# Scaled copies out of the gates' banks, and three pieces of side work moved by a few tiles

## The chip, the cores and the metric

The kernel runs on one core of a Trainium2 chip. The metric is the device time of one execution, in microseconds (us). A core has five engines that run their own instruction queues in order: PE (matmuls; its weight loads are listed as PEld), DVE (elementwise work on tensors), ACT (activations, copies, casts), POOL (here memsets and masks) and SP (here it only starts DMAs). They wait for each other by semaphores.

## The reference

One decoder layer on 256 tokens of width 2048, all float32. The parts that the change touches:

```python
h = rmsnorm(x, norm_gain[l])
z = h @ w_in[l]
(gq, gk_, gv, ggate, gdown, fq, fk, fv, flogit, fgate, mq, mgate, merge) = jnp.split(z, IN_OFFSETS, axis=-1)
gk_log = jax.nn.log_sigmoid((gdown @ w_gk_up[l] + b_gk[l]).astype(jnp.float32)) / GK_NORMALIZER
o_a = gla_chunked(...)                                   # gated linear attention, 4 heads of 256
o_a = rmsnorm(o_a, gla_norm_gain[l]).reshape(B, S, GLA_WIDTH).astype(x.dtype)
o_a = o_a * jax.nn.silu(ggate)
log_f = jax.nn.log_sigmoid((flogit + b_f[l]).astype(jnp.float32))
o_b = forgetting_attention(...) * jax.nn.silu(fgate)
mkv = rmsnorm(mem, mem_norm_gain[l]) @ w_mem_kv[l]       # 256 memory tokens
o_c = memory_attention(...) * jax.nn.silu(mgate)
gates = jax.nn.sigmoid(merge.reshape(B, S, N_BRANCH, D))
y = gates[:, :, 0] * (o_a @ wb_a) + gates[:, :, 1] * (o_b @ wb_b) + gates[:, :, 2] * (o_c @ wb_c)
x = x + y @ w_out[l]
return rmsnorm(x, final_gain)
```

Here `gdown` has 16 columns and `flogit` 8: these 24 are the "small columns". Norms are not applied to x or mem before the products: the products are made with the raw x times the gain, and their results are scaled afterwards by the token's reciprocal root mean square (`xcol`, `xrow` for x, `mcol`, `mrow` for the memory tokens; a column has a token on a partition, a row has the tokens along the free axis, the same on all partitions).

## The kernel before

The 2048 input rows are 16 tiles of 128, the "kts". All large weights are streamed in 34 blocks of 2048 rows by 512 columns, in the fixed order of a table: gq, gk, gv (two blocks), fq, fk, fv, the memory's k and v, mq, ggate (two blocks), fgate, mgate, then four times three merge blocks and one block of the branches, and four blocks of the output projection. A float32 weight is loaded (`raw`), cast to a high part by ACT (`hi`, L174, in the first block L130), and the rest is subtracted by DVE (`lo`, L187, in the first block L131). Each product is made of three: high by high, high by low, low by high. The casts and subtractions work in pieces of two kts, which run three and two pieces ahead of PE. The first block is special: x itself comes with it, so `first_piece` (L376) loads x and weights piece by piece, and splits both.

Blocks are computed in two ways. `natural` (L211) has the tokens on the partitions: for each kt and each of the two token tiles three matmuls, into two PSUM banks (L224 to L226). `transposed` (L232) has the columns on the partitions, four banks: in groups of four kts each bank c in turn gets a 512-wide matmul (L255) and a 256-wide one (L257) for each kt; at the end a bank is emptied by an ACT copy (L240) and a DVE addition (L243). There are four `acc` banks for these blocks and four `att` banks for the rest (and for gq, which is in groups of one kt). A block that follows reuses the banks of the one before it, so its first matmul on a bank waits for whoever empties that bank.

All other work is written as generators in three lanes, `post`, `side` and `main`. After each kt (in groups of four: after each bank's turn) `pull` advances each lane by one step. A generator that yields n is taken up again n pulls later. So the numbers in `yield` fix where an instruction stands in its engine's queue, and since each lane is a list, what follows in a lane moves with it.

The change touches these: `small` (L411), first in the side lane: splits the small columns `wsr` in two halves of eight kts (L422, L423) and multiplies them (L431: eight matmuls for kts 0 to 7, then four, then four); `wsr` and the 16 rows of the low-rank weight `w3r` are loaded in `first_piece` (L398 to L400). After it in the side lane stand the scale of x (`scale_first`, L502), the loads and splits of the memory tokens (`load_mem`, L365), and the memory tokens' scale: `rms_of` (L298: four squares on ACT, L308; then the sums on DVE, L311 and L312; then `rsqrt`, L285, with Ln and Exp on ACT, each of which needs a table load, L290 and L291) and `row_of` (L315: a DVE multiplication of the identity, L319, a matmul by ones, L322, a copy). In the main lane `gla_decay` (L526) makes three stacked copies `z3` of the small result and multiplies them (L543); the scores with L658, L661 and L662 follow. `silu_gate` (L895) is for the two ggate blocks: natural product, then `evac`, a sigmoid of the scaled PSUM bank by ACT (L902, with a table load ahead of it), the product of bank, scale and sigmoid by DVE (L904, which frees the bank), and four products with the attention's result (L910).

Of the kernel before, what the change touches and what calls it, by code (L numbers as in the profile page):

```python
# [12 lines left out]
AF = mybir.ActivationFunctionType  # L13
ALU = mybir.AluOpType
AX = mybir.AxisListType

P = 128
# [43 lines left out]
def body(ctx, tc, xT, memT, xn, memn, wall, wsm, wup, cst, fgain, out):  # L61
# [250 lines left out]
        nc.vector.tensor_scalar(ms, ms, 4.0 / D, 4 * EPS, ALU.mult, ALU.add)  # L312
        yield from rsqrt(col, ms, NT)

    def row_of(col, row):  # L315

        dg = a2([P, NT, P])
        for t in range(NT):
            nc.vector.tensor_scalar(dg[:, t, :], ident, col[:, t:t + 1], None, ALU.mult)  # L319
        yield 2  # L320
        ps = att()
        MM(ps[:, :S], lhsT=ones, rhs=dg.rearrange("p t s -> p (t s)"), start=True, stop=True)  # L322
        yield 1
        nc.scalar.copy(row, ps[:, :S])
        yield 1
# [53 lines left out]
    def first_piece(g, s, raw, hi, lo):  # L379

        if s == 0:
            xraws.append(a4([P, 4, S]))
            x12.append(new_h("x12_", g))
        step = 1 if g < 2 else 2
        for k in range(0, 2, step):
            ks = slice(2 * s + k, 2 * s + k + step)
            kts = slice(4 * g + ks.start, 4 * g + ks.stop)
            nc.sync.dma_start(xraws[g][:, ks, :], xT[:, kts, :])
            cut = (0, 256, NB) if kts.start == 0 else (0, NB)
            for a, b in zip(cut, cut[1:]):  # L390
                nc.sync.dma_start(raw[:, ks, a:b], wall[0, :, kts, a:b])
            for j in range(ks.start, ks.stop):
                kt = 4 * g + j
                high_x(x12[g], xraws[g][:, j, :], j, cs[:, C_GAIN + kt:C_GAIN + kt + 1])
                low_x(x12[g], xraws[g][:, j, :], j, cs[:, C_GAIN + kt:C_GAIN + kt + 1])
                for a, b in zip(cut, cut[1:]):
                    split_w(raw[:, j, a:b], hi[:, j - 2 * s, a:b], lo[:, j - 2 * s, a:b])
        if (g, s) == (1, 1):  # L398
            nc.sync.dma_start(wsr, wsm)
            nc.sync.dma_start(w3r, wup)  # L400

# [8 lines left out]
    def small():  # L410

        for g in range(2):
            z0 = a4([P, 8, P], F32)
            nc.gpsimd.memset(z0, 0.0)
            ws = a4([P, 8, P], F32R)
            nc.gpsimd.tensor_copy(ws, z0)
            zs.append(ws)
        yield 3
        for g in range(2):
            ws, wr = zs[g], wsr[:, 8 * g:8 * g + 8, :]  # L420
            for (a, b, wdt) in ((0, 0, 16), (32, 16, 8)):
                nc.vector.tensor_copy(ws[:, :, a:a + wdt], wr[:, :, b:b + wdt])  # L422
                nc.vector.tensor_tensor(out=ws[:, :, 64 + a:64 + a + wdt], in0=wr[:, :, b:b + wdt],  # L423
                                        in1=ws[:, :, a:a + wdt].bitcast(F32), op=ALU.subtract)
            yield 3
        nc.scalar.copy(w3, w3r)
        nc.vector.tensor_tensor(out=w3[32:64], in0=w3r[32:64], in1=w3[32:64].bitcast(F32), op=ALU.subtract)
        sp = acc()
        for kts, n in ((range(0, 8), 3), (range(8, 12), 4), (range(12, 16), 1)):
            for kt in kts:  # L430
                MM(sp, lhsT=zs[kt // 8][:, kt % 8, :], rhs=h_of(x12, kt).rearrange("p a s -> p (a s)"),  # L431
                   start=(kt == 0), stop=(kt == KT - 1))
            yield n
        nc.scalar.copy(sm, sp[0:64, S:])
        nc.vector.tensor_tensor(out=sm, in0=sp[0:64, :S], in1=sm, op=ALU.add)
        nc.vector.tensor_tensor(out=sm, in0=sp[64:128, :S], in1=sm, op=ALU.add)
        yield 1
# [89 lines left out]
    def gla_decay():  # L527
# [7 lines left out]
        nc.scalar.copy(z3[0:32], sm[0:32])  # L535
        nc.scalar.copy(z3[32:64], sm[0:32])
        nc.vector.tensor_tensor(out=z3[64:96], in0=sm[0:32], in1=z3[0:32].bitcast(F32), op=ALU.subtract)
        yield 1
        for c in range(2):
            ps = att()  # L540
            for j in range(2):
# [353 lines left out]
    def silu_gate(dst, rstd):  # L895
# [1 line left out]
        ps = natural(x12, range(KT), w_kts(w_block()))  # L897

        def evac():
            sgs = [a2([P, NB]) for _ in range(NT)]  # L900
            for t in range(NT):
                nc.scalar.activation(sgs[t], ps[t], AF.Sigmoid, scale=xcol[:, t:t + 1])  # L902
            for t in range(NT):
                nc.vector.scalar_tensor_tensor(out=sgs[t], in0=ps[t], scalar=xcol[:, t:t + 1], in1=sgs[t],  # L904
                                               op0=ALU.mult, op1=ALU.mult)
                yield 1
            for t in range(NT):
                for j in range(2):
                    sl = slice(j * 256, (j + 1) * 256)
                    nc.vector.scalar_tensor_tensor(out=dst(t)[:, sl], in0=dst(t)[:, sl],  # L910
                                                   scalar=rstd()[:, t, j:j + 1], in1=sgs[t][:, sl],
                                                   op0=ALU.mult, op1=ALU.mult)
                yield 1
            yield 1

        return evac()

# [26 lines left out]
    side.append(load_mem())  # L944
    side.append(gap(10))
    side.append(rms_of(memn, mcol, lambda: a4([P, 1024])))
    side.append(row_of(mcol, mrow))
    G["k"] = proj_T(x12, scaled(lambda: G["row"]))
    main.append(gla_decay())
    main.append(gla_scores())  # L950
# [258 lines left out]
```

## Time and profile before

| what | value |
| --- | --- |
| median of three runs | 817.73 us (817.65 to 817.75) |
| profiled execution | 817.97 us, of which the span of the instructions is 816.0 us |
| mean granted clock of PE | 0.998 |
| PE busy | 802.0 us (98%) in 3888 matmul records |
| DVE / ACT / POOL busy | 499.4 (61%) / 408.6 (50%) / 22.1 us (3%) |
| HBM | 154.55 MB read, 192 GB/s over the span |

In rows of the timeline the first number is the start in us from the start of the span, the second the duration in us; then come the engine, the line of the kernel, the operation, what it writes and reads, shapes and types, how many instructions are put together in the row, and in square brackets the idle time of the engine just before it and who ended it. In the list of waits: who waited for whom, us in total, how often, the longest in us. In a table of windows a row has the stretch, its length, the busy time (and number of instructions) of PE, PEld, DVE, ACT and POOL, then the granted clock of PE (1.00 is full speed), the busy share of the DMA engines and GB/s. In a group of instructions: how many, busy us and mean ns of one, idle us before.

### The profile page before, as it was taken

What the parts mean: (1) busy time and instruction counts of PE and PEld (TensorE: products, weight loads), DVE (VectorE), ACT (ScalarE), POOL (GpSimd) and SP (SyncE); (2) the same over time, 40 slices, a digit from 0 to 9 for tenths busy, and PEclk for the clock granted to TensorE, in tenths of its full rate; (3) what the DMA queues carried; (4) which work ended last, traced back from release to release, by engine and by line L of the source; (5) the groups of instructions that cost most, each with busy time, mean ns of one, the idle gap of its engine ahead of it and who ended that gap; (6) DMA issues with size and microseconds to landing.
All of it is one profiled execution on the core that took longest, in us unless ns stands there. A gap on an engine that the chain in (4) does not pass through costs nothing.

```text
span 816.0 us, 9964 instructions
## 1 busy us (share of the span) xinstructions
PE 802.0 (98%) x3888; PEld 673.0 (82%) x3888; DVE 499.4 (61%) x705; ACT 408.6 (50%) x560; POOL 22.1 (3%) x44
## 2 busy tenths in 40 slices
PE   8999999999999999999999999999999999999995
PEld 7888888788888787888888888888888888888885
DVE  6767978875756575567445644474446544575653
ACT  6777745744645464555444444434444444444631
POOL 6000010100000000000000000000000000000000
PEclk9999999999999999999999999999999999999999
DMA  8965646643444443555555455555555555548633
GB/s 294 368 235 181 239 158 237 213 161 130 180 155 156 156 153 123 187 182 186 200 206 187 173 206 197 178 193 203 180 188 203 183 184 200 206 161 308 233 125 103
DMA packets 27439, 157.31 MB, mean 193 GB/s; under 512 B 3216, under 2 KB 4640, under 8 KB 10496
## 3 DMA queue, kind: packets, MB, share of 16 engines
q1 hardware_dynamic: 27120, 156.64, 54.0%
q8 instruction: 30, 0.49, 0.2%
q14 instruction: 17, 0.14, 0.0%
q10 hardware_dynamic: 144, 0.02, 0.0%
q0 software_dynamic: 128, 0.02, 0.0%
HBM read 154.55 MB, written 2.10 MB: 192 GB/s over the span
## 4 chain that ended last, share of the span: by engine, by line
PE 60%; DVE 1%; ACT 0%; DVEq 0%; issue 0%
PE acc L226 14%; PE acc L224 14%; PE acc L225 14%; PE acc L1073 4%; PE acc L1074 4%; PE acc L1075 4%; PE acc L255 3%; PE acc L257 2%; PE att L986 0%; PE att L844 0%; DVE b L904 0%; DVE lo L187 0%; PE att L888 0%; PE att L853 0%; PE att L862 0%; ACT b L902 0%
## 5 line engine op out<-in xcount | busy, mean ns | idle before, releaser
L187 DVE TENSOR_TENSOR lo<-raw,hi 128x1024 fp32r<-128x1024 f32 x256 | 312.2, 1223 | 199.7 <-ACT hi L174 199.5
L174 ACT CAST hi<-raw 128x1024 fp32r<-128x1024 f32 x256 | 265.8, 1050 | 318.0 <-PE acc L226 237.9
L224 PE MATMUL acc<-hi,x 128*128 128x512 f32 x544 | 215.2, 396 | 0.0
L225 PE MATMUL acc<-lo,x 128*128 128x512 f32 x544 | 212.1, 390 | 0.0
L226 PE MATMUL acc<-hi,x 128*128 128x512 f32 x544 | 212.1, 390 | 0.0
L255 PE MATMUL acc<-x,hi 128*128 128x512 f32 x384 | 138.9, 404 | 1.3 <-DVE b L904 1.2
L226 PEld LDWEIGHTS acc<-hi,x 128*128 128x128 f32 x544 | 102.1, 188 | 21.6
L225 PEld LDWEIGHTS acc<-lo,x 128*128 128x128 f32 x544 | 102.2, 188 | 21.0 <-DVE lo L187 0.5
L224 PEld LDWEIGHTS acc<-hi,x 128*128 128x128 f32 x544 | 102.2, 188 | 21.0 <-issue 0.3
L257 PE MATMUL acc<-x,lo 128*128 128x256 f32 x384 | 107.3, 280 | 0.0
L255 PEld LDWEIGHTS acc<-x,hi 128*128 128x128 f32 x384 | 72.1, 188 | 18.4 <-DVE b L904 1.9
L257 PEld LDWEIGHTS acc<-x,lo 128*128 128x128 f32 x384 | 72.4, 189 | 0.5 <-DVE lo L187 0.2
L226 PE MATMUL acc<-hi,oT 128*128 128x512 f32 x128 | 49.8, 389 | 0.0
L225 PE MATMUL acc<-lo,oT 128*128 128x512 f32 x128 | 49.8, 389 | 0.0
L224 PE MATMUL acc<-hi,oT 128*128 128x512 f32 x128 | 49.8, 389 | 0.0
L1073 PE MATMUL acc<-hi,a 128*128 128x512 f32 x96 | 37.6, 391 | 0.0
L1075 PE MATMUL acc<-hi,a 128*128 128x512 f32 x96 | 37.4, 390 | 0.0
L1074 PE MATMUL acc<-lo,a 128*128 128x512 f32 x96 | 37.4, 389 | 0.0
L225 PEld LDWEIGHTS acc<-lo,oT 128*128 128x128 f32 x128 | 24.0, 188 | 5.0
L226 PEld LDWEIGHTS acc<-hi,oT 128*128 128x128 f32 x128 | 24.0, 188 | 5.0
L224 PEld LDWEIGHTS acc<-hi,oT 128*128 128x128 f32 x128 | 24.0, 188 | 5.0
L255 PE MATMUL att<-x,hi 128*128 128x512 f32 x64 | 24.1, 415 | 0.6 <-ACT hi L130 0.6
(223 smaller groups left out, 803.2 us busy)
## 6 DMA issues: line engine op xcount, KB each, us to landing
raw<-wall SPq DMA_DIRECT2D x130, 1024.0 KB, 4.7
a<-xn SPq DMA_DIRECT2D x8, 512.0 KB, 7.2
raw<-wall SPq DMA_DIRECT2D x4, 512.0 KB, 6.9
a<-memT SPq DMA_DIRECT2D x4, 512.0 KB, 7.4
a<-memn SPq DMA_DIRECT2D x4, 512.0 KB, 7.5
lraw<-wall SPq DMA_DIRECT2D x2, 1024.0 KB, 7.4
out<-a SPq DMA_DIRECT2D x8, 256.0 KB, 3.1
raw<-wall SPq DMA_DIRECT2D x7, 256.0 KB, 4.8
```

The lines of the kernel that those rows point to most:

```text
L174: nc.scalar.copy(hi, raws[q][:, 2 * s:2 * s + 2, :])
L187: nc.vector.tensor_tensor(out=lo, in0=raws[q][:, 2 * s:2 * s + 2, :], in1=parts[n][0].bitcast(F32), op=ALU.subtract)
L224: MM(ps[t], lhsT=h1, rhs=hi, start=(kt == first), stop=False)
L225: MM(ps[t], lhsT=h1, rhs=lo, start=False, stop=False)
L226: MM(ps[t], lhsT=h2, rhs=hi, start=False, stop=(kt == last))
L255: MM(ps[c], lhsT=hi[:, cs_], rhs=hk.rearrange("p a s -> p (a s)"), start=(kt == 0), stop=False, skip_group_check=True)
L257: MM(ps[c][:, :S], lhsT=lo[:, cs_], rhs=hk[:, 0, :], start=False, stop=(kt == KT - 1), skip_group_check=True)
L1073: MM(ps, lhsT=h1, rhs=hi, start=(kt == 0), stop=False)
L1074: MM(ps, lhsT=h1, rhs=lo, start=False, stop=False)
L1075: MM(ps, lhsT=h2, rhs=hi, start=False, stop=(kt == KT - 1))
```

## The change

Five edits. In `row_of` the distance between the DVE multiplication and the matmul becomes a parameter, 2 as before for the tokens' scale and 6 for the memory tokens'. In `first_piece` the loads of the small columns move from behind the piece of kts 6 and 7 to behind the piece of kts 10 and 11. In `small` the splits are six pulls after the start rather than three, and one pull apart rather than three, which makes the side lane one pull shorter up to the matmuls L431. In `gla_decay` the matmuls come two pulls after the copies rather than one, and all of the main lane behind them one pull later. In `evac` of the gates the bank is emptied by an ACT copy with the scale (a Copy needs no table here), the product with the attention's result is made from that copy, and the sigmoid is taken of the copy in place afterwards and multiplied in.

```diff
--- before.py
+++ after.py
@@ -312,12 +312,12 @@
         nc.vector.tensor_scalar(ms, ms, 4.0 / D, 4 * EPS, ALU.mult, ALU.add)
         yield from rsqrt(col, ms, NT)
 
-    def row_of(col, row):
+    def row_of(col, row, wait=2):
 
         dg = a2([P, NT, P])
         for t in range(NT):
             nc.vector.tensor_scalar(dg[:, t, :], ident, col[:, t:t + 1], None, ALU.mult)
-        yield 2
+        yield wait
         ps = att()
         MM(ps[:, :S], lhsT=ones, rhs=dg.rearrange("p t s -> p (t s)"), start=True, stop=True)
         yield 1
@@ -395,7 +395,7 @@
                 low_x(x12[g], xraws[g][:, j, :], j, cs[:, C_GAIN + kt:C_GAIN + kt + 1])
                 for a, b in zip(cut, cut[1:]):
                     split_w(raw[:, j, a:b], hi[:, j - 2 * s, a:b], lo[:, j - 2 * s, a:b])
-        if (g, s) == (1, 1):
+        if (g, s) == (2, 1):
             nc.sync.dma_start(wsr, wsm)
             nc.sync.dma_start(w3r, wup)
 
@@ -415,14 +415,14 @@
             ws = a4([P, 8, P], F32R)
             nc.gpsimd.tensor_copy(ws, z0)
             zs.append(ws)
-        yield 3
+        yield 6
         for g in range(2):
             ws, wr = zs[g], wsr[:, 8 * g:8 * g + 8, :]
             for (a, b, wdt) in ((0, 0, 16), (32, 16, 8)):
                 nc.vector.tensor_copy(ws[:, :, a:a + wdt], wr[:, :, b:b + wdt])
                 nc.vector.tensor_tensor(out=ws[:, :, 64 + a:64 + a + wdt], in0=wr[:, :, b:b + wdt],
                                         in1=ws[:, :, a:a + wdt].bitcast(F32), op=ALU.subtract)
-            yield 3
+            yield 1
         nc.scalar.copy(w3, w3r)
         nc.vector.tensor_tensor(out=w3[32:64], in0=w3r[32:64], in1=w3[32:64].bitcast(F32), op=ALU.subtract)
         sp = acc()
@@ -535,7 +535,7 @@
         nc.scalar.copy(z3[0:32], sm[0:32])
         nc.scalar.copy(z3[32:64], sm[0:32])
         nc.vector.tensor_tensor(out=z3[64:96], in0=sm[0:32], in1=z3[0:32].bitcast(F32), op=ALU.subtract)
-        yield 1
+        yield 2
         for c in range(2):
             ps = att()
             for j in range(2):
@@ -897,21 +897,23 @@
         ps = natural(x12, range(KT), w_kts(w_block()))
 
         def evac():
-            sgs = [a2([P, NB]) for _ in range(NT)]
+            zs = [a2([P, NB]) for _ in range(NT)]
             for t in range(NT):
-                nc.scalar.activation(sgs[t], ps[t], AF.Sigmoid, scale=xcol[:, t:t + 1])
-            for t in range(NT):
-                nc.vector.scalar_tensor_tensor(out=sgs[t], in0=ps[t], scalar=xcol[:, t:t + 1], in1=sgs[t],
-                                               op0=ALU.mult, op1=ALU.mult)
-                yield 1
+                nc.scalar.activation(zs[t], ps[t], AF.Copy, scale=xcol[:, t:t + 1])
+            yield 2
             for t in range(NT):
                 for j in range(2):
                     sl = slice(j * 256, (j + 1) * 256)
                     nc.vector.scalar_tensor_tensor(out=dst(t)[:, sl], in0=dst(t)[:, sl],
-                                                   scalar=rstd()[:, t, j:j + 1], in1=sgs[t][:, sl],
+                                                   scalar=rstd()[:, t, j:j + 1], in1=zs[t][:, sl],
                                                    op0=ALU.mult, op1=ALU.mult)
                 yield 1
-            yield 1
+            for t in range(NT):
+                nc.scalar.activation(zs[t], zs[t], AF.Sigmoid)
+            yield 2
+            for t in range(NT):
+                nc.vector.tensor_tensor(out=dst(t), in0=dst(t), in1=zs[t], op=ALU.mult)
+                yield 1
 
         return evac()
 
@@ -944,7 +946,7 @@
     side.append(load_mem())
     side.append(gap(10))
     side.append(rms_of(memn, mcol, lambda: a4([P, 1024])))
-    side.append(row_of(mcol, mrow))
+    side.append(row_of(mcol, mrow, 6))
     G["k"] = proj_T(x12, scaled(lambda: G["row"]))
     main.append(gla_decay())
     main.append(gla_scores())
```

How the order of the instructions changes is shown at three places. The first is DVE in the first block: L351 is the low part of x, L131 that of the weights (two of each per piece of two kts), L422 and L423 the splits of `wsr`, first half `a_191` (now `a_189`), second half `a_195` (now `a_193`). Before:

```order
L351 SCALAR_TENSOR_TENSOR x_30_209<-a_208,cs,x_30_209 128x256
L131 TENSOR_TENSOR lo_207<-raw_205,hi_206 128x512
L422 CAST a_191<-wsr 128x8x16
L423 TENSOR_TENSOR a_191<-wsr,a_191 128x8x16
L422 CAST a_191<-wsr 128x8x8
L423 TENSOR_TENSOR a_191<-wsr,a_191 128x8x8
L351 SCALAR_TENSOR_TENSOR x_30_209<-a_208,cs,x_30_209 128x256
L131 TENSOR_TENSOR lo_241<-raw_205,hi_240 128x512
```

and now, where `lo_266` is the piece of kts 12 and 13:

```order
L351 SCALAR_TENSOR_TENSOR x_37_268<-a_267,cs,x_37_268 128x256
L131 TENSOR_TENSOR lo_266<-raw_264,hi_265 128x512
L422 CAST a_189<-wsr 128x8x16
L423 TENSOR_TENSOR a_189<-wsr,a_189 128x8x16
L422 CAST a_189<-wsr 128x8x8
L423 TENSOR_TENSOR a_189<-wsr,a_189 128x8x8
L422 CAST a_193<-wsr 128x8x16
L423 TENSOR_TENSOR a_193<-wsr,a_193 128x8x16
L422 CAST a_193<-wsr 128x8x8
L423 TENSOR_TENSOR a_193<-wsr,a_193 128x8x8
```

The first half's split stood behind kt 9's low parts and now stands behind kt 13's, with the second half's right after it. On PE the first eight matmuls L431 stand behind kt 8, where they stood behind kt 9:

```order
L255 MATMUL att_184<-x_30_207,hi_204 128x512
L257 MATMUL att_184<-x_30_207,lo_205 128x256
L431 MATMUL acc_331<-x_8_114,a_189 128x512 x4
L431 MATMUL acc_331<-x_15_148,a_189 128x512 x4
L255 MATMUL att_175<-x_30_207,hi_204 128x512
L257 MATMUL att_175<-x_30_207,lo_205 128x256
```

The second place is ACT at the end of the fk block, where the memory tokens' scale is made: L308 are the squares, L240 the copies that empty fk's banks (`acc_1280` the first, `acc_1295` the second; now `acc_1280` and `acc_1296`), L290 and L291 the Ln and Exp with their table loads. Before:

```order
L308 ACTIVATE a_1424,ssq_1306<-a_1424 128x1024
L662 ACTIVATE a_1464<-a_1464 128x768
L240 COPY a_1275<-acc_1280 128x256
L308 ACTIVATE a_1426,ssq_1306<-a_1426 128x1024
L240 COPY a_1275<-acc_1295 128x256
L290 ACT_TABLE_LOAD
L290 ACTIVATE nwp_1520<-ms_1517 128x2
L291 ACT_TABLE_LOAD
L291 ACTIVATE nwp_1520<-nwp_1520 128x2
L240 COPY a_1275<-acc_1311 128x256
```

and now:

```order
L658 ACTIVATE a_1449<-a_1449 128x1024
L308 ACTIVATE a_1402,ssq_1289<-a_1402 128x1024
L240 COPY a_1275<-acc_1280 128x256
L290 ACT_TABLE_LOAD
L290 ACTIVATE nwp_1504<-ms_1501 128x2
L291 ACT_TABLE_LOAD
L291 ACTIVATE nwp_1504<-nwp_1504 128x2
L662 ACTIVATE a_1477<-a_1477 128x768
L240 COPY a_1275<-acc_1296 128x256
L240 COPY a_1275<-acc_1311 128x256
```

The last square now stands ahead of the first copy, and both table loads with L662 ahead of the second. The third place is ACT at the end of the second ggate block (`acc_2627` and `acc_2628`, now `acc_2625` and `acc_2626`). Before:

```order
L174 CAST hi_2838<-raw_2713 128x1024
L902 ACT_TABLE_LOAD
L902 ACTIVATE b_2849<-acc_2627,xcol 128x512
L902 ACTIVATE b_2850<-acc_2628,xcol 128x512
L174 CAST hi_2897<-raw_2771 128x1024
```

and now:

```order
L174 CAST hi_2838<-raw_2703 128x1024
L902 ACTIVATE b_2849<-acc_2625,xcol 128x512
L902 ACTIVATE b_2850<-acc_2626,xcol 128x512
L868 ACTIVATE b_2826,msum<-att_2825,mmx 128x256 x2
L174 CAST hi_2895<-raw_2758 128x1024
L174 CAST hi_2897<-raw_2758 128x1024
L912 ACT_TABLE_LOAD
L912 ACTIVATE b_2849<-b_2849 128x512
L912 ACTIVATE b_2850<-b_2850 128x512
```

The table load and the sigmoids have moved behind two casts, and only copies stand between the block's end and the free banks.

## The prediction

> **What bounds the kernel now.** I read the page first, then the waits of PE, then the timeline around each of them.
>
> ```profile
> span 816.0 us, 9964 instructions
> PE 802.0 (98%) x3888; PEld 673.0 (82%) x3888; DVE 499.4 (61%) x705; ACT 408.6 (50%) x560; POOL 22.1 (3%) x44
> PE 60%; DVE 1%; ACT 0%; DVEq 0%; issue 0%
> PE att L322 <- DVE b L319: 1.4, 1, 1.4
> PE acc L255 <- DVE b L904: 1.2, 1, 1.2
> PE att L255 <- ACT hi L130: 0.6, 1, 0.6
> PE att L257 <- DVE lo L131: 0.4, 2, 0.2
> PE att L543 <- ACT hi L174: 0.2, 1, 0.2
> ```
>
> PE is busy for 802.0 of 816.0 us, and the chain of waits lies on it. The change neither adds nor removes a matmul, so only PE's stalls can move. The four lines of waits below L322's, and that one, are the places the change touches; all of them together hold about 4 us. Any stall that the change makes is paid in full, since nothing behind PE has to catch up.
>
> **The change, part by part.**
>
> *A. The small columns.* Their loads go two pieces back and the first half's splits eight DVE instructions back, while the small matmuls L431 come one kt earlier on PE.
>
> ```profile
> 8.98 0.48 SPq L399 DMA_DIRECT2D wsr<-wsm  x1
> 10.71 0.43 SPq L388 DMA_DIRECT2D a<-xT  x1
> 14.07 0.33 SPq L391 DMA_DIRECT2D raw<-wall  x1
> 17.26 0.28 PE L257 MATMUL att<-x,lo 128*128 128x256 f32 x1
> 21.41 0.62 ACT L130 CAST hi<-raw 128x512 fp32r<-128x512 f32 x1
> 22.35 0.61 ACT L130 CAST hi<-raw 128x512 fp32r<-128x512 f32 x1
> 23.95 0.69 DVE L131 TENSOR_TENSOR lo<-raw,hi 128x512 fp32r<-128x512 f32 x1
> 19.73 0.22 DVE L422 CAST a<-wsr 128x128 fp32r<-128x128 f32 x1
> 20.42 0.23 DVE L423 TENSOR_TENSOR a<-wsr,a 128x64 fp32r<-128x64 f32 x1
> 21.57 2.00 PE L431 MATMUL acc<-x,a 128*128 128x512 f32 x8
> 23.41 0.39 PE L255 MATMUL att<-x,hi 128*128 128x512 f32 x1
> 27.64 1.08 PE L431 MATMUL acc<-x,a 128*128 128x512 f32 x4
> ```
>
> Today SP issues wsr's load at 8.98 and wup's after it, so the xT of kts 8 and 9 is issued only at 10.71. Without those two, kt 8's data comes 10.71 − 8.98 = 1.7 us sooner, and the stall before kt 8 (0.6 for the cast, some 0.2 twice for lo) goes: kt 7's last matmul starts at 17.26, and kt 8 would run from about 17.4 to 18.8 (one kt takes (27.64 − 23.41)/3 = 1.41). That is the gain meant.
>
> Behind kt 8, however, L431 now stands, and it needs the first half's split of wsr. On DVE this split has moved behind the lo pieces up to kt 13. So PE waits for kt 13's weights before it may do kt 9, which is ready. Kt 12 and 13's weights are issued at 14.07 today; the two loads moved still stand ahead of them, so they come no earlier. ACT casts kt 12 at 21.41 and kt 13 at 22.35, ending 22.96. Then lo of kt 13 (0.69, to 23.7) and the split of the first half (19.73 to 20.65: 0.92) follow, to 24.6, and L431 starts at about 24.7. If lo of kt 13 stays where it is today (23.95) it is 25.6; if the casts come half a microsecond earlier, 24.1.
>
> L431 started at 21.57 with kts 8 and 9 done; now it starts at 24.7 with kt 8 alone done. So A costs (24.7 − 21.57) + 1.41 = **+4.5 us** (3.9 to 5.4), the removed stall counted in. PE then stands idle for 24.7 − 18.8 = 5.9 us, where DVE and ACT work on, so all later splits lie readier than today and no further stall follows. The second half's split comes right behind and is ready by 25.6; its four matmuls stand three kts later.
>
> *The clock.* So long an idle stretch brings the granted clock in.
>
> ```profile
> 1.13 3.35 PE L343 MATMUL att<-ones 128*128 128x128 f32 x14 [1.13 <-DVE ones L335]
> 5.24 0.63 PE L255 MATMUL att<-x,hi 128*128 128x512 f32 x1
> 7.04 0.40 PE L255 MATMUL att<-x,hi 128*128 128x512 f32 x1
> 807.02 0.28 PE L1075 MATMUL acc<-last,a 128*128 128x256 f32 x1
> 812.00:812.50 0.50, 0.00 (x0) 0.00 (x0) 0.00 (x0) 0.00 (x0) 0.00 (x0) 0.92 1.00 279
> 812.50:814.00 1.50, 0.00 (x0) 0.00 (x0) 0.00 (x0) 0.00 (x0) 0.00 (x0) 0.50 0.60 202
> ```
>
> The last matmul ends at 807.3. The granted clock (the column before the last two) is 0.92 on average from 812.0 to 812.5 and 0.50 after, so it fell at 812.4, 5.1 us after the end of work. At the start, matmuls run from 1.13; a 512-wide one still takes 0.63 at 5.24 and 0.40 at 7.04, so full speed came some 5 to 6 us after the first. An idle stretch of 5.9 us is longer than 5.1, so I expect the clock to halve just before L431. Slow work costs about 1 − 0.40/0.63 = 37% to half of its time, say 45%. Five and a half slow microseconds would cost 2.5; as L431 follows soon after the fall and the first slow period at the start followed no earlier work, between half of it and all: **+2.0** (0, if the clock does not fall in time, to 2.8).
>
> The Trainium skill, page "TensorE: Matmul & The Clock Gate", section "Part 1: The HAM clock gate (the "warmup" mystery)", has the gate closed by a whole idle window of about 3.4 us and opened by a busy one, the windows running free. By that rule 5.9 us of idle hold a whole window in (5.9 − 3.4)/3.4, about 70%, of all alignments, and the closed clock lasts one to two windows, an estimate of 1.5 to 3 us lost; the 5.1 us at the end agree with it.
>
> *B. The memory tokens' scale.* L322 now stands three kts further back on PE, so its wait of 1.4 goes. But the side lane is one step earlier in all that follows the small columns, and the table loads of mcol's rsqrt now stand ahead of a copy that frees a bank.
>
> ```profile
> 146.14 2.00 ACT L174 CAST hi<-raw 128x1024 fp32r<-128x1024 f32 x2 [0.44 <-PE acc L255]
> 148.04 1.06 ACT L308 ACTIVATE a<-a 128x1024 f32<-128x1024 f32 x1
> 148.37 1.22 DVE L661 TENSOR_TENSOR a<-a,a 128x1024 f32<-128x1024 f32 x1
> 149.10 0.83 ACT L662 ACTIVATE a<-a 128x768 f32<-128x768 f32 x1
> 150.64 0.42 DVE L243 TENSOR_TENSOR a<-acc,a 128x256 f32<-128x256 f32 x1
> 151.13 0.35 ACT L240 COPY a<-acc 128x256 f32<-128x256 f32 x1
> 151.51 1.28 ACT L290 ACT_TABLE_LOAD   x1
> 153.02 1.28 ACT L291 ACT_TABLE_LOAD   x1
> 152.26 0.39 PE L224 MATMUL acc<-hi,x 128*128 128x512 f32 x1
> 153.01 0.19 PEld L224 LDWEIGHTS acc<-hi,x 128*128 128x128 f32 x1 [0.33 <-DVE a L243]
> ```
>
> Today both copies L240 of fk's first two banks are done by 151.5, ahead of the loads, and fv's second bank opens at 153.01 with a wait of 0.33. In the new order ACT does, from the end of the two casts at 148.1 (bound by PE, so they stay): L308, L658, L308 (1.06 each, L658 of the same shape, to 151.3), L240 (0.35, to 151.65), the loads with Ln and Exp (from the start of the first load today to the end of the second 153.02 + 1.28 − 151.51 = 2.8, and Exp with it some 3.0, to 154.6), L662 (0.83, to 155.4), and only then the second L240 (to 155.8). DVE's L243 (0.42) then opens fv's second bank at about 156.2. DVE itself stands at L311 until the last L308, then L661 and a lo (1.22 each) keep the first bank's L243 until 154.6; PE waits there first, from 152.26, and the rest of the wait at the second bank. So the second bank opens at 156.2 in place of 153.0: +3.2 − 1.4 = **+1.8 us** (from −1.4, if the loads hide as they do today, to +2.4).
>
> *C. The gates.* Today a table load and two sigmoids from PSUM stand before L904, which frees the banks.
>
> ```profile
> 316.63 1.28 ACT L902 ACT_TABLE_LOAD   x1
> 319.44 0.50 PE L255 MATMUL acc<-x,hi 128*128 128x512 f32 x1 [1.17 <-DVE b L904]
> 321.24 0.19 PEld L255 LDWEIGHTS acc<-x,hi 128*128 128x128 f32 x1 [0.45 <-DVE b L904]
> L471 ACT ACTIVATE a<-acc,xcol 128x512 f32<-128x512 f32 x6 | 4.0, 678 | 0.0
> ```
>
> The scaled copy is of the form of L471, 0.68 each. From 316.63 the copies free the banks at 317.3 and 318.0; PE wants the first at 319.44 − 1.17 = 318.3 and the second later. Both waits go, 1.17 + 0.45: **−1.6 us** (0, if something else keeps the banks, to −1.6). The table load, the sigmoids in place (four more ACT instructions in all, 0.68 each by the same row) and the multiplication by DVE come later, beside PE's next block; ACT is busy for 50% of the span, and the transposes that want the result stand kts later. Without that cover a late result would cost what the gate's chain grows by, 2 × 0.68 and a second DVE pass, about 2 us.
>
> *D. The decay's matmuls* L543 move one kt back; their wait of 0.2 goes: **−0.2**. The rest of main's lane goes one kt later with them, which moves work past other banks' copies, at no more than ±0.5 by the size of the waits quoted.
>
> Sum: 4.5 + 2.0 + 1.8 − 1.6 − 0.2 = +6.5. The profiled execution took 817.97 us (span 816.0), 0.24 over the median 817.73, so 824.5 in its own time and **824.2 us** beside the median.
>
> **The rivals.** *First, the bank is not held:* ACT reaches the loads with time to spare because fk's banks fill later than I place them, and B is −1.4. For it: L308 waits for nothing today. Against it: the order puts 3.0 us of table work straight ahead of a copy that PE stands 0.33 behind already. 817.7 + 4.5 + 2.0 − 1.4 − 1.6 − 0.2 = 821.0.
>
> *Second, the clock does not fall:* idle time and fall lie 0.8 us apart, and the end of the program may differ from its middle. For that: one fall only is on the trace. Against: the three times agree within 0.1 us, though each holds a slow start where each microsecond of shift would show as 0.4; so the clock's steps do not wander. 824.2 − 2.0 = 822.2; with B gained too 819.0, close to no difference.
>
> *Third, the clock's whole price and late ends everywhere:* L431 at 25.6, 2.8 slow: 817.7 + 5.4 + 2.8 + 1.8 − 1.6 − 0.2 = 825.9.
>
> *Fourth, on the other side, the change does what it says:* the split of wsr is not late, for instance since PE's wait is released by an earlier count than that behind kt 13. Then the stall before kt 8 (0.6 + 0.4), L322's 1.4, the gate's 1.6 and 0.2 go: 817.7 − 4.2 = 813.5. With those gains it decides where L431 waits for less than 4.2, that is, starts before 18.8 + 4.2 = 23.0. Against it stands the row of lo at 23.95 with the split of the second half right behind it today, which shows that DVE cannot be there sooner.
>
> **How the numbers follow.** My forecast (A, clock, B and C as summed) 0.52, with a range of its own of 822.0 to 825.6; the first rival 0.15; the second 0.15, a third of it with B gained; the third 0.10; the fourth 0.08. The likeliest gives 824.2. The range leaves out the fourth and the far ends: 819.2 to 826.4. Differences under 0.2%, 1.6 us, are about what a measurement of this kernel can't tell from none. Faster holds the fourth, 0.08; no difference holds the second rival with B gained, 0.05, and a little of the first, 0.07 in all; slower the rest, 0.85.
>
> **What would show it.** In the new profile the waits of PE should have as their longest line L431 behind DVE's split L423, 5 to 6 us, beginning near 19 and ending near 24.7; the granted clock should drop below 1.00 shortly before and be back within about 6 us; L224 should wait for L243, 2 to 3 us in two pieces near the start of fv; L322, L543 and L255 behind the gate should be gone from the list. The forecast is wrong if L431's wait is under 3 us, if the clock stays 1.00, or if the fv block opens without a wait.

## The result, and the profile after

The changed kernel took 827.05 us (median; 826.54 to 828.07), the kernel before 817.74 (817.65 to 818.87): a ratio of 1.0109, 95% interval 1.0096 to 1.0122, so 9.3 us slower. The profiled execution took 827.03, with a span of 825.0 and a mean granted clock of 0.990. The prediction was 824.2 with a range to 826.4: the sign and the main wait came as forecast, the time lies above the range.

The head of the page and the list of PE's waits after the change (the first matmul's wait for L335 at the start stands in both kernels):

```profile
span 825.0 us, 9975 instructions
PE 805.8 (98%) x3888; PEld 676.7 (82%) x3888; DVE 500.3 (61%) x705; ACT 410.7 (50%) x564; POOL 22.1 (3%) x44
PE acc L431 <- DVE a L422: 5.9, 1, 5.9
PE acc L224 <- DVE a L243: 2.6, 2, 1.8
PE att L343 <- DVE ones L335: 1.1, 1, 1.1
PE acc L255 <- ACT a L471: 0.7, 1, 0.7
```

All waits that the change aimed at are gone from the list: L322, L904, L543 and those before kt 8. One that it did not aim at is gone too; before the change the list had it as

```profile
PE att L853 <- DVE b L873: 0.2, 1, 0.2
```

Three others stand there now, 9.2 us in all, where those that are gone held 4.0. PE is also busy 3.8 us longer with the same number of matmuls.

The first block in the timeline (ACT's cast and DVE's lo of kt 13, the first half's split, and the two groups of L431):

```profile
22.55 0.60 ACT L130 CAST hi<-raw 128x512 fp32r<-128x512 f32 x1
23.27 0.68 DVE L131 TENSOR_TENSOR lo<-raw,hi 128x512 fp32r<-128x512 f32 x1
23.87 0.22 DVE L422 CAST a<-wsr 128x128 fp32r<-128x128 f32 x1
24.93 3.75 PE L431 MATMUL acc<-x,a 128*128 128x512 f32 x8 [5.87 <-DVE a L422]
33.62 1.11 PE L431 MATMUL acc<-x,a 128*128 128x512 f32 x4
```

and the windows around it and around the start of fv (last three numbers: granted clock, DMA share, GB/s):

```profile
20.00:22.00 2.00, 0.00 (x0) 0.00 (x0) 1.08 (x2) 0.89 (x2) 1.06 (x2) 1.00 1.06 412
22.00:24.00 2.00, 0.00 (x0) 0.00 (x0) 1.74 (x4) 2.00 (x5) 0.00 (x0) 0.92 1.04 428
24.00:26.00 2.00, 1.07 (x3) 0.91 (x4) 1.86 (x10) 1.61 (x4) 0.00 (x0) 0.50 1.00 414
30.00:32.00 2.00, 2.00 (x11) 1.72 (x11) 0.03 (x1) 1.05 (x1) 0.00 (x0) 0.87 0.96 393
162.00:163.00 1.00, 0.60 (x3) 0.17 (x1) 0.09 (x1) 1.00 (x3) 0.00 (x0) 1.00 0.82 164
163.00:164.00 1.00, 0.61 (x2) 0.50 (x3) 0.34 (x1) 1.00 (x3) 0.00 (x0) 0.82 0.88 352
164.00:165.00 1.00, 1.00 (x4) 0.81 (x3) 0.87 (x1) 1.00 (x3) 0.00 (x0) 0.50 1.02 434
167.00:168.00 1.00, 1.00 (x5) 0.84 (x5) 0.96 (x4) 0.66 (x1) 0.00 (x0) 0.98 0.00 0
```

The split stands behind kt 13's lo, so PE waits 5.87 us and starts L431 at 24.93. The clock falls at 23.69 (0.92 on average from 22 to 24) and is back at 30.51. Eight matmuls L431 take 3.75 in place of 2.00, and the distance from the first L431 to the next group, with the same matmuls between, is 33.62 − 24.93 = 8.69 where it was 27.64 − 21.57 = 6.07. The clock falls a second time, at 163.63, for 3.4 us, just behind the waits at fv's banks:

```profile
158.50 0.35 ACT L240 COPY a<-acc 128x256 f32<-128x256 f32 x1
158.63 0.16 DVE L311 TENSOR_TENSOR ms<-ssq 128x2 f32<-128x2 f32 x1 [2.76 <-ACT a L308]
158.87 1.28 ACT L290 ACT_TABLE_LOAD   x1
159.60 0.28 PE L257 MATMUL acc<-x,lo 128*128 128x256 f32 x1
160.39 1.28 ACT L291 ACT_TABLE_LOAD   x1
161.17 0.42 DVE L243 TENSOR_TENSOR a<-acc,a 128x256 f32<-128x256 f32 x1
161.64 0.50 PE L224 MATMUL acc<-hi,x 128*128 128x512 f32 x1 [1.77 <-DVE a L243]
161.79 0.83 ACT L662 ACTIVATE a<-a 128x768 f32<-128x768 f32 x1
162.53 0.62 ACT L240 COPY a<-acc 128x256 f32<-128x256 f32 x2
163.39 0.62 PE L224 MATMUL acc<-hi,x 128*128 128x512 f32 x1 [0.79 <-DVE a L243]
163.81 0.63 PE L225 MATMUL acc<-lo,x 128*128 128x512 f32 x1
```

DVE waits at L311 for the last square, so the first bank's L243 comes at 161.17; ACT comes to the second bank's copy at 162.53, behind two table loads and L662. Measured from the start of one matmul to the start of the next, PE loses 1.93 and 0.96 us at the two banks. Behind them a matmul such as L225 takes 0.63, and the next starts 0.43 after it in place of 0.23.

The third new wait is at mq's third bank, which held a result of the memory's v; ACT empties it by L471 only after four activations L776 of the main lane. The last three lines are at the second ggate block, whose banks are free in time:

```profile
247.14 0.50 ACT L776 ACTIVATE b<-b,fmx 128x256 f32<-128x256 f32 x1
247.41 0.28 PE L257 MATMUL acc<-x,lo 128*128 128x256 f32 x1
247.63 1.24 ACT L471 ACTIVATE a<-acc,mcol 128x512 f32<-128x512 f32 x2
248.35 0.50 PE L255 MATMUL acc<-x,hi 128*128 128x512 f32 x1 [0.67 <-ACT a L471]
327.22 1.26 ACT L902 ACTIVATE b<-acc,xcol 128x512 f32<-128x512 f32 x2
327.30 0.28 PE L257 MATMUL acc<-x,lo 128*128 128x256 f32 x1
327.42 0.40 PE L255 MATMUL acc<-x,hi 128*128 128x512 f32 x1
```

The two copies L902 take 1.26 and PE goes through without a stop.

| place | predicted | from the two traces |
| --- | --- | --- |
| A, wait at L431, net (24.93 − 21.57 + 1.41) | +4.5 | +4.8 |
| clock behind it (8.69 − 6.07) | +2.0 | +2.6 |
| B, fv's banks 1.93 + 0.96, less L322's 1.57 | +1.8 | +1.3 |
| clock behind fv's banks, 8 matmuls 0.20 late each | none | +1.6 |
| L471 at mq's third bank | within ±0.5 | +0.8 |
| C, gate (1.33 + 0.30) | −1.6 | −1.6 |
| D, L543; and L853 | −0.2; none | −0.4; −0.4 |
| sum | +6.5 | +8.7 |

The profiled executions differ by 827.03 − 817.97 = 9.06; 0.4 us are not placed.

### The profile page after: what moved, and what is told of

The parts are those of the page before. It is cut to its first block, busy times and chain, and to the rows that moved or that the text cites. A ratio compares the mean times of both kernels' runs of the same rounds, so it can differ in the third digit from the quotient of the medians.

```text
span 825.0 us, 9975 instructions
## 1 busy us (share of the span) xinstructions
PE 805.8 (98%) x3888; PEld 676.7 (82%) x3888; DVE 500.3 (61%) x705; ACT 410.7 (50%) x564; POOL 22.1 (3%) x44
## 4 chain that ended last, share of the span: by engine, by line
PE 69%; ACT 0%; DVE 0%; DVEq 0%; issue 0%
PE acc L224 16%; PE acc L225 16%; PE acc L226 16%; PE acc L255 5%; PE acc L1077 4%; PE acc L1075 4%; PE acc L1076 4%; PE acc L257 3%; PE att L988 0%; PE att L844 0%; PE att L862 0%; PE att L799 0%; PE att L787 0%; PE att L888 0%; PE att L853 0%; PE att L764 0%
## 5 line engine op out<-in xcount | busy, mean ns | idle before, releaser
L224 PE MATMUL acc<-hi,x 128*128 128x512 f32 x544 | 215.7, 397 | 2.6 <-DVE a L243 2.6
L225 PE MATMUL acc<-lo,x 128*128 128x512 f32 x544 | 212.6, 391 | 0.0
L224 PEld LDWEIGHTS acc<-hi,x 128*128 128x128 f32 x544 | 102.6, 189 | 24.4 <-DVE a L243 3.3
L225 PEld LDWEIGHTS acc<-lo,x 128*128 128x128 f32 x544 | 102.5, 188 | 20.4
L224 PE MATMUL acc<-hi,oT 128*128 128x512 f32 x128 | 49.8, 389 | 0.0
L225 PE MATMUL acc<-lo,oT 128*128 128x512 f32 x128 | 49.8, 389 | 0.0
L224 PEld LDWEIGHTS acc<-hi,oT 128*128 128x128 f32 x128 | 24.0, 188 | 5.0
L225 PEld LDWEIGHTS acc<-lo,oT 128*128 128x128 f32 x128 | 24.0, 188 | 5.0
```

Of the source, the lines that this page charges most:

```text
L224: MM(ps[t], lhsT=h1, rhs=hi, start=(kt == first), stop=False)
L225: MM(ps[t], lhsT=h1, rhs=lo, start=False, stop=False)
```

## The experiments

Each ratio is to runs of the kernel before that were made beside the run. These 69 runs had medians of 818.5 (e1 to e4), 818.3 (e5 to e8), 818.5 (e9 to e12) and 818.0 (e13, e14), where it was 817.74 beside the changed kernel, and they range from 817.2 to 820.9. So a difference between the medians of two kernels that were not run side by side can be off by some 0.8 us. In a diff, - and + are against the kernel that the text names.

**The side lane's step (e1_gap), against the changed kernel:**

```diff
-    side.append(gap(10))
+    side.append(gap(11))
     side.append(rms_of(memn, mcol, lambda: a4([P, 1024])))
```

> The changed kernel with the memory tokens' scale one pull later in the side lane (gap of 11 in place of 10), all else as changed. The order then has both copies L240 of fk's first two banks ahead of the two table loads again. Theory: the side lane's step cost the waits at fv's two banks (1.93 + 0.96 us between matmuls) and, with them, the halved clock just behind (about 1.6 us); both go, and L322 still waits for nothing: 827.05 - 2.9 - 1.6 = 822.5. Rival: the waits come from the main lane's shift in gla_decay, or DVE is late by itself; then they stay and the time is within 1 us of 827.0.

Measured: 824.27 (822.72 to 824.64), ratio to before 1.0063 (1.0040 to 1.0086). Among its waits of PE:

```profile
PE acc L431 <- DVE a L422: 6.3, 1, 6.3
PE att L687 <- DVE a L612: 0.6, 1, 0.6
PE att L687 <- DVE a L701: 0.4, 1, 0.4
```

The wait of L224 is gone, and the clock is 1.00 at fv. So neither comes without the side lane's step, and the rival falls. But the gain between medians is 2.8 and not 4.5: two waits of L687 (0.79 and 0.58 between starts), which fv's late banks had covered, came up, and L431 waited 0.4 longer in this profile.

**The clock (e2_filled), against the changed kernel:**

```diff
         sp = acc()
+        for _ in range(24):
+            MM(sp, lhsT=x12[0][:, 0, 0, 0:P], rhs=x12[0][:, 0].rearrange("p a s -> p (a s)"),
+               start=True, stop=True)
```

> The changed kernel with 24 additional matmuls of 128x512 ahead of L431, into the same bank (their result is overwritten): they fill the wait of 5.9 us and end before the split is ready. Theory: the wait itself stays (L431 at 24.9), but the clock stays at 1.00 through the first block, and the slow stretch from 23.7 to 30.5, 2.6 us lost, goes: 824.4. Rival: the slow matmuls behind the wait are due to the DMAs and splits that run there, not to the idle stretch: no change, 827.0.

Measured: 824.19 (823.59 to 824.69), ratio 1.0065 (1.0048 to 1.0083). In its windows and timeline (the added matmuls are its L430, the small ones its L434):

```profile
24.00:26.00 2.00, 1.86 (x9) 1.25 (x8) 1.86 (x10) 1.16 (x4) 0.00 (x0) 1.00 1.02 424
26.00:28.00 2.00, 2.00 (x12) 1.65 (x11) 1.97 (x5) 1.10 (x3) 0.00 (x0) 1.00 0.66 274
19.32 5.61 PE L430 MATMUL acc<-x 128*128 128x512 f32 x24
25.07 1.16 PE L434 MATMUL acc<-x,a 128*128 128x512 f32 x4
```

The small matmuls start at 25.07, no sooner than without the filling (24.93), DVE and the DMAs are as busy as in the changed kernel, and the clock stays at 1.00 there: 2.9 us gained between medians, where 2.6 were expected. The slow stretch is the idle time's, not the traffic's.

**Both waits filled (e13_filled2), against the kernel of e2_filled:**

```diff
+    for _ in range(4):
+        fill = att()
+        for _ in range(2):
+            MM(fill, lhsT=x12[0][:, 0, 0, 0:P], rhs=x12[0][:, 0].rearrange("p a s -> p (a s)"),
+               start=True, stop=True)
     fv = proj_N(x12, xcol)
```

> The changed kernel with the first block's wait filled by 24 additional matmuls, and fv's first wait by 8 more into four banks that are then free (all results unused). Theory: the wait at fv's first bank is filled, that at the second (about 0.9) stays, and no window is idle for most of its length, so the clock stays 1.00 throughout: 1.6 less than with the first filling alone (824.2), so 822.6. Rival: fv's slow stretch is not the idle time's doing: 824.2.

Measured: 823.75 (822.36 to 823.98), ratio 1.0066 (1.0049 to 1.0082), no clear difference from 824.19. The clock is 1.00 from its first rise to the end of the work, as the theory has it; around fv's start:

```profile
160.00:162.00 2.00, 1.30 (x5) 0.48 (x3) 0.68 (x2) 1.99 (x6) 0.00 (x0) 1.00 0.53 123
162.00:164.00 2.00, 1.92 (x8) 1.61 (x9) 1.20 (x3) 2.00 (x3) 0.00 (x0) 1.00 0.94 393
```

The wait at the second bank is still there (0.94 between starts). In the profile the first small matmul comes at 26.22, 1.15 later than in e2_filled's, which hides the gain in the whole time: PE is 1.14 us behind e2_filled's when the first block resumes, still 1.14 up to fv's start, and 0.46 ahead of it behind the clock's fall there (0.64 in the end). So fv's stretch gained 1.14 + 0.46 = 1.6 us within the two traces, as expected. The mean granted clock of all four runs, 0.996 to 0.998 against 0.994 to 0.996 in e2_filled, agrees; the medians do not show the gain, so it stands on traces.

**The first half's split, earlier (e3_split4), against the changed kernel:**

```diff
-        yield 6
+        yield 4
...
-            yield 1
+            yield 2
         nc.scalar.copy(w3, w3r)
```

> The changed kernel with the first half's split two pulls earlier (yield 4, then 2 and 2; the matmuls L431 stay where the change put them, behind kt 8; the side lane keeps its shorter length). The split then stands behind kt 11's low parts. Theory: L431 waits from 18.9 to about 21.6, so 3.3 us less, and since the clock's window then holds work for more than half of its length, it does not fall: 2.6 more; the waits at fv stay: 827.05 - 3.3 - 2.6 = 821.1. Rival: a wait of 2.7 us halves the clock too, and a window's share does not matter: about 823.

Measured: 822.23 over eight runs (820.59 to 826.33), ratio 1.0054 (1.0034 to 1.0073): between the two theories. The profile was taken in the slowest run. There L431 waited 3.5 us (to 24.3) and the clock fell at 24.28 for 3.4 us; at fv it fell for 6.8 us:

```profile
158.00:160.00 2.00, 0.23 (x3) 0.02 (x1) 1.93 (x3) 1.97 (x3) 0.52 (x1) 1.00 0.01 2
160.00:162.00 2.00, 1.21 (x4) 0.74 (x5) 0.42 (x1) 1.99 (x6) 0.00 (x0) 0.70 0.67 172
162.00:164.00 2.00, 2.00 (x5) 1.54 (x6) 1.54 (x2) 1.65 (x3) 0.00 (x0) 0.50 0.83 352
166.00:168.00 2.00, 2.00 (x7) 1.53 (x6) 2.00 (x5) 1.76 (x2) 0.00 (x0) 0.59 0.00 0
```

The wait was 0.8 longer than I had worked out: in this profile the weights of kts 10 and 11 landed 9.2 us after their issue, at 20.5, and lo of kt 11 ended at 23.0. The spread of 5.7 us over eight runs of one kernel is itself a reading. The mean granted clock was 0.994 in the three fastest and 0.990 to 0.991 in the three slowest, so the clock was low for longer in the slow ones; only one run has a trace that shows where.

**The same with L431 behind kt 9 and the lane's length as before (e4_split4_10), against the changed kernel:**

```diff
-        yield 6
+        yield 4
...
-            yield 1
+            yield 3 - g
         nc.scalar.copy(w3, w3r)
```

> The same, but with the matmuls L431 one pull later (yield 4, then 3 and 2), so behind kt 9 as before the change, and the side lane as long as before the change. Theory: L431 starts at about 21.6 as before the change (no gain, no loss there), the waits at fv go with the lane's length, the gains at L322 (1.6), at the gate (1.6), at L543 and L853 (0.4 each) stay, and the new wait behind L471 (0.8) too: 817.7 - 1.6 - 1.6 - 0.8 + 0.8 = 814.5. Rival: the waits at fv are the main lane's: 4.5 more, 819.

Measured: 816.77 (816.04 to 820.38), ratio 0.9984 (0.9969 to 0.9999): just faster than before, 2.3 us short of the theory. L431 still waits 1.4, fv's waits are gone and the clock does not fall; the two waits of L687 (0.76 and 0.58) are there as in e1_gap and take back 1.3 of the missing 2.3, and L431 starts 0.3 later than before the change, at 21.91.

**The main lane's step taken back (e14_gap_decay), against the kernel of e1_gap:**

```diff
-        yield 2
+        yield 1
         for c in range(2):
             ps = att()
```

> The changed kernel with the memory tokens' scale one pull later (as in the run with a gap of 11, 824.3) and gla_decay's yield back at 1. Theory: the main lane's step makes both L471's wait (0.83) and the two of L687 (0.79 and 0.58) that appeared when fv's wait was mended; all go and L543's 0.38 comes back: 824.3 - 2.2 + 0.4 = 822.5. Rival: L687 waits since mcol's work has moved, not the main lane: its two waits stay, 823.9.

Measured: 821.08 (819.38 to 821.49), ratio 1.0036 (1.0023 to 1.0049), 3.2 under e1_gap. Its list of PE's waits is down to two lines:

```profile
PE acc L431 <- DVE a L422: 5.8, 1, 5.8
PE att L343 <- DVE ones L335: 1.1, 1, 1.1
```

L471's wait and both of L687 are gone with the main lane's step, so they were its doing. What remains of the loss is the wait in the first block with its slow clock; no other new wait is in the list.

**The parts alone, each against the kernel before.** e5_gate has the change's `evac`; e6_row6 has the parameter of `row_of` at 6 for the memory tokens; the others:

```diff
 e7_decay, before the loop over L543:
-        yield 1
+        yield 2
 e8_loads:
-        if (g, s) == (1, 1):
+        if (g, s) == (2, 0):
 e11_gap9:
-    side.append(gap(10))
+    side.append(gap(9))
 e12_small: the change's two edits in small and first_piece
```

> The kernel before with the gates' edit alone (scaled copies empty the banks, sigmoid in place later). Theory: the waits of fgate's first matmuls behind the gate (1.33 and 0.30 us between matmuls) go and nothing comes for them: 817.7 - 1.6 = 816.1. Rival: something else keeps the banks or the later sigmoid makes the transposes late: 817.7 or more.

> The kernel before with the wait of 6 in row_of for the memory tokens alone. Theory: L322's 1.57 us go, since nothing wants the row for many kts: 816.2. Rival: the row's copy or who uses it is late in turn: 817.7.

> The kernel before with gla_decay's yield 2 alone, which moves the whole main lane one kt back. Theory: L543's 0.38 and L853's 0.41 go, but ACT then stands at the four L776 when mv's banks are to be emptied by L471, and mq's third bank opens 0.8 us late: together 817.7 (within 0.3). Rival: the L471 wait comes from another edit, and the yield gains its 0.8: 816.9.

> The kernel before with the loads of the small columns behind the piece of kts 8 and 9 (the splits unmoved, which is as far as the loads can go with them). Theory: the stall before kt 8 (0.77 + 0.49 us) goes, and the splits still find wsr landed: 817.7 - 1.3 = 816.5. Rival: the data of kts 10 and 11 are late in its place, or the split waits for wsr: 817.7.

> The kernel before with the memory tokens' scale one pull earlier in the side lane (gap of 9 in place of 10) and nothing else: the table loads then stand ahead of the copy that empties fk's second bank. Theory: fv's second bank opens 2.2 us late, L322's 1.57 gets shorter by up to as much as PE is behind: between 818.5 and 820.5 against 818.3, with a wait of L224 behind L243 of 2 us or more in the profile; the clock stays, as the idle stretch is one and short. Rival: the main lane's shift is needed for the wait: no L224 wait over 0.5 us.

> The kernel before with the edits of the small columns alone, as the change has them (loads behind kts 10 and 11, yields 6, 1 and 1). Theory: the wait at L431 of 5.9 us, 4.8 net, the slow stretch behind it, 2.6, and a wait at fv's second bank in place of part of L322's, 0 to 2: 818.3 + 7.4 + (0 to 2) = 826 to 828, which is all of the change's loss and more. Rival: the loss needs the other edits too: under 824.

| run | median (range), us | ratio to before (95%) |
| --- | --- | --- |
| e5_gate | 815.97 (815.37 to 816.54) | 0.9972 (0.9961 to 0.9983) |
| e6_row6 | 816.86 (815.99 to 819.33) | 0.9984 (0.9975 to 0.9992) |
| e7_decay | 819.67 (819.18 to 821.97) | 1.0020 (1.0012 to 1.0029) |
| e8_loads | 817.62 (816.71 to 818.81) | 0.9994 (0.9985 to 1.0002) |
| e11_gap9 | 819.56 (818.19 to 822.24) | 1.0013 (1.0002 to 1.0024) |
| e12_small | 826.98 (824.88 to 828.02) | 1.0092 (1.0073 to 1.0112) |

The gate's part and `row_of`'s gain 2.4 and 1.5 us, about what their waits say (2.0 with L853's 0.4, which goes with the gate's part, and 1.6). The loads gain 0.7 of the 1.3 expected, inside the noise, though the stall before kt 8 is gone from the profile. `gla_decay`'s step costs 1.3 by itself; two of its waits show why my 0 was wrong:

```profile
PE att L322 <- DVE b L319: 2.4, 1, 2.4
PE acc L255 <- ACT a L471: 0.7, 1, 0.7
```

L471's wait is there with this edit alone, and L322's grows from 1.4 to 2.4, as DVE comes to L319 later. The side lane one step earlier alone (e11_gap9) makes fv's second bank late with no other edit; the wait at the first bank does not come with it. Against my expectation the clock fell:

```profile
PE acc L224 <- DVE a L243: 1.9, 1, 1.9
154.00:156.00 2.00, 0.62 (x3) 0.54 (x4) 0.42 (x1) 1.99 (x6) 0.00 (x0) 1.00 1.02 430
156.00:158.00 2.00, 2.00 (x7) 1.52 (x6) 1.81 (x5) 2.00 (x4) 0.00 (x0) 0.52 0.04 10
```

The edits of the small columns alone (e12_small), which also make the side lane one step shorter, are 8.5 us slower than before. L224's line in its list is that of e11_gap9, and the clock falls twice in its profile, in the wait of L431 and behind that of L224:

```profile
PE acc L431 <- DVE a L422: 6.8, 1, 6.8
```

Alone, the other parts come to −2.4 − 1.5 + 1.3 = −2.6, so the parts do not simply add up to the change's 9.3. One reason is in the lists: L322 waits for nothing in e12_small either, so `row_of`'s 1.5 can't be gained a second time. The rest of the difference was not traced.

**A version of the parts that gain (e9_kept, e10_kept_d).** Against the kernel before: the gates' edit, `row_of` with 6, the loads at (2, 0); e10_kept_d also has `yield 2` before L543's loop and leaves out the `yield 1` ahead of the log-sigmoid, so the main lane keeps its length.

> The kernel before with three of the parts, in forms that leave both lanes as long as they were: the gates' edit, the wait of 6 in row_of, and the loads of the small columns behind the piece of kts 8 and 9 (splits, small matmuls and gla_decay unmoved). Theory: the parts add up, since their stalls lie in different blocks: against 818.3 on this chip 2.2 for the gate with L853 (1.63, 0.30, 0.41 less what overlaps), 1.5 for L322, 0.7 for the loads: about 814.0, and no drop of the clock. Rival: a gain in one place comes back as a wait in the next (as L687's did behind fv): over 815.5.

> The same, and in gla_decay the yield of 2 ahead of L543, but with the later yield ahead of the log-sigmoid taken out, so that the main lane behind is as long as before the change. Theory: L543's wait of 0.38 goes and neither L471 nor L322 nor L687 waits more: 0.4 under the run before it in this call. Rival: the change of order in those few instructions makes lo pieces late in the 80s of the span, where DVE has no slack: no gain or some tenths lost.

Measured: 813.88 (813.17 to 814.23), ratio 0.9940 (0.9928 to 0.9953), and 813.43 (812.78 to 814.72), ratio 0.9938 (0.9923 to 0.9952): both some 5 us faster than the kernel before and 13 than the change. Whether the last edit adds anything is not settled. In e10_kept_d's profile L543's wait is replaced by a wait for a lo piece, as its rival had it:

```profile
PE acc L225 <- DVE lo L187: 0.3, 1, 0.3
```

## Why the prediction was wrong

*What bounds the kernel* held: PE's waits, read from the list, moved the time, and those that the prediction named went or came where the order said.

*A* held, in mechanism and size: 5.9 us of wait at 19 to 24.9 as predicted, 4.8 net against 4.5. e14_gap_decay shows that it is what remains of the loss when the lanes are set right; e12_small, that the edits of the small columns, with the side lane's step that comes with them, are enough for a loss of 8.5.

*The clock* was a right mechanism with too small a price: 2.6 against 2.0. I took a middle between half of the slow time at the start and all of it. By e2_filled it is 2.9 between medians. The slow stretch lasted 6.8 us, longer than the 5 to 6 that I bounded it by.

*B* had the mechanism right (wait 2.9 against 3.2, in two pieces as said; by e1_gap there is none without the side lane's step, and by e11_gap9 the step alone is enough for the one at the second bank, 2.1 between starts, though not for the one at the first). The step that failed is that the sum charged the clock only to the first block. At fv the idle stretches were 1.9 and 1.0 us, well under the 5.1 that I took from the end of the program as the length which halves the clock, and the clock fell all the same: 1.6 us that the sum did not have. One observation of a fall gave an upper bound for the length that it needs, and I used it as the length itself.

*The main lane's step* (in D) was the other that failed: "no more than ±0.5" for all that moves with it. It is 0.8 at L471 in the change, 1.3 for the edit alone, and two waits of L687 more once fv's wait does not cover them. I had looked through the places where blocks change for banks emptied late, and missed the one where ACT empties mv's banks behind L776.

*C* held (−1.6; −2.4 alone, with L853). *D* was −0.4.

*The rivals.* The first, second and fourth fell with the wait of L224, the clock's fall and the wait of L431. The third, 825.9, came nearest, but by a late L431 (25.6 against the measured 24.93) and not by what failed. Against the second I gave a wrong reason: the three runs before agree within 0.1 us, and I took this to show that the clock's steps do not wander. That agreement was luck: a fourth run took 818.87, and the 69 later ones range over 3.7 us. In the sixteen profiles of this case the clock reaches full speed at the start between 4.0 and 7.3 us. How much of the spread comes from that is not shown; in the profiles of e6_row6 and e8_loads, where it comes early (4.9), waits for the first kts' data stand in the place of the slow matmuls.

Between 6.5 and 9.06 lie: +1.6 for the second fall, +0.8 for L471, +0.6 for the first fall, +0.3 for A, −0.5 for B and −0.6 for L543 and L853, in all +2.2; 0.4 stay open.

## What to carry to other kernels

A step in a lane of generators moves all that follows it: look for every bank that is emptied behind the moved work, above all where table loads come to stand ahead of a copy. A wait on the busy engine costs more than its length: if PE is idle for more than half of some 3.4 microseconds, its work right behind can be slow for as long again or twice as long, and this belongs to the sum of every such wait. When a wait is mended, look for the next one that it covered.

## What the runs showed of the hardware

The granted clock changes on a grid of 3.41 us: in every trace with several changes these lie whole multiples of it apart (in the changed kernel at 6.62, 23.69, 30.51, 163.63 and 167.05 us, the last four 5, 7, 46 and 47 steps behind the first). Where the grid lies differs from run to run, and with it what a wait costs: in e14_gap_decay's profile the clock fell at 20.91, 3.8 us before the end of a wait of 5.8, and was back 3.0 us after it; in the changed kernel it fell 1.2 before the end and stayed low for 5.6 after it.

A stretch of this grid need not be idle for the clock to fall. PE was busy for 1.2 of the 3.41 us before the fall at 163.63 (35%), for 1.4 in e14_gap_decay before its fall at 20.91 (41%), and for 1.5 in e11_gap9 and e12_small, 1.6 in e2_filled and 1.65 in e3_split4 (44, 44, 47 and 48%) before theirs at fv. With 46% twice (e1_gap, 17.7 to 21.1, and e11_gap9, 808.0 to 811.4), 50% (the kernel before, 805.6 to 809.0), 51% (e12_small, 814.5 to 817.9) and 59% or more it stayed. So in these traces it turns somewhat below half, with no sharp bound: 46% stayed where 47 and 48% fell, and the matmuls' ends are modelled. The way back needs more: at the half clock, stretches with PE busy for 64% (the changed kernel, 23.69 to 27.10), 71% (e1_gap, from 24.50) and 77% (e3_split4, from 160.82) did not bring the full clock back, and one with 88% (e14_gap_decay, from 24.32) did.

The Trainium skill, page "TensorE: Matmul & The Clock Gate", section "Part 1: The HAM clock gate (the "warmup" mystery)", gives the window of about 3.4 us, free-running, and one idle window as the condition of the fall. Grid and free run agree with these traces. That the window must be idle does not: stretches in which PE was busy for 35 to 48% ended in a fall too. By that condition the waits at fv would have cost nothing beyond their length.
